# The mixer of a two-layer decoder trunk on one core: the spacing of the chains' steps on TensorE, the queue place of the transposed shares' copies, and the time at which gated outputs are turned

## The chip, the cores and the metric

The kernel runs on one core of a Trainium2 chip. The metric is device time in microseconds (us) of one execution; lower is better. The kernel before takes 2161.09 us, the median of three runs from 2160.48 to 2162.0.

## The reference

Two layers; x has 512 tokens of 1024 features, float32 throughout. Each layer is a feed-forward half-step, a mixer, and a second feed-forward half-step, each between RMS norms:

```python
for l in range(DEPTH):
    x = x + 0.5 * rms_norm(swiglu(rms_norm(x, gn[0]), w_gate, w_up, w_down), gn[1])
    proj = rms_norm(x, gn[2]) @ w_in[l]
    hq, hf, hi, hg, aq, ak, av, gate_a, gate_b = jnp.split(proj, IN_SPLITS, axis=-1)
    y_hg = hgrn2_mixer(hq, hf, hi, hg, lb_all[l], hgrn_head_gain[l]) @ w_branch_hgrn[l]
    y_at = swa_sink_attention(aq, ak, av, attn_sinks[l]) @ w_branch_attn[l]
    mixed = jax.nn.sigmoid(gate_a) * y_hg + jax.nn.sigmoid(gate_b) * y_at
    x = x + rms_norm(mixed @ w_out[l], gn[3])
    ...
```

`hgrn2_mixer` is a gated linear recurrence with four heads of 128 by 128 state; each head's output is divided by its own root mean square and multiplied by the SiLU of `hg`. `swa_sink_attention` is attention of eight heads over a window of 128 tokens with a distance penalty and a sink in the softmax; it is computed in four blocks of 128 queries. Only the mixer is touched by the change.

## The kernel before

Every large product is done in three TensorE products of a high and a low part (`mm3`), since one pass in the fast float32 format isn't exact enough. Weights arrive by DMA on SP's queue in tiles of 128 by 1024, ScalarE rounds the high part (`whi`, L228), and the low part (`wlo`) is made by VectorE (L235) or by an accumulating DMA on GpSimd's queue (L232, L233). Activations stay in SBUF in a pool of 61 slots named `s`. PSUM has eight banks: five named `acc` for the main stream, three named `aux` for the chains below. An `aux` bank can be written anew only when the last reader of the tile that held it is done.

**What sets the order.** TensorE's instructions stand in the order in which the code issues them. Those of the other engines are put in order by a scheduler when the program is built; each engine then works through its list in that order, and the order in the built program is the one that the chip runs.

In the mixer (`mixer`, L837) there is a main stream of projections and several chains that run beside it, written as generators. The main stream gives, in order: the projections for the first two recurrence heads (`quad`), the keys, queries and values of the attention, two token-major projections (`project_tok`: the recurrence's values `vs`, copied out at L991, and the out-gates `gs`, L995 to L998), the last two heads' projections, eight attention branches (`branch`), and then the recurrence branches (`branches`), the last of which ask for the whole of the attention (`attended`) and of the recurrence (`recurred`). The chains are four heads (`head`, its steps in `run` and `recurrence_scores`) and two attention chains, which take blocks 0 and 2, and 1 and 3 (`attend`).

`Order` keeps an estimated TensorE time `t`: `mm` and `transpose` add to it. A chain yields a number of ns from the table `WAIT` when it must wait for other engines; after each weight block of the main stream (`wmm`: three products) `poll` steps every chain that is due. `until` steps the chains without any main product between, while a result is missing.

The steps that the prediction names:

- An attention block: scores on TensorE (12 products of 64 rows per step, two steps); VectorE adds the distances (L925), reduces the maximum (L930, L932) and prepares the softmax (L934, L936); ScalarE takes eight exponentials (L942) with their sums `den`; VectorE inverts `den` (L946, L947) and scales the shares (L950, four instructions). Then for each of up to two key blocks eight TensorE transposes fill two `aux` banks (L111), ScalarE copies both out (L963), and after both key blocks four products use the copies as moving operands (L104, `aux<-s,s` with 64 columns); L972 and L974 split the result.
- A head's end: ten products of 128 by 128 into one `aux` bank, ScalarE squares (L866), VectorE sums (L868), ScalarE takes the root (L869), VectorE inverts (L870) and scales out of the bank (L872). After `norm` ns the gates are multiplied in (L877, four instructions of 128 by 128), after `gate` ns four transposes turn the gated output.

```python
    po = aux()
    for t in range(TT):
        for s in range(t + 1):
            mm(po[:, t * P : (t + 1) * P], block(s, t), vs[s][:, i * P : (i + 1) * P], s == 0, s == t)
    ...
    yield WAIT["gate"]
```

- Ahead of a head's end, two products make its last cross-chunk scores (`s2`), which ScalarE copies out (L825) and which the head's end then reads; the time between is `blocks` (350 ns).
- `sums` (L451, then L353 to L356 and the split at L303 and L304) prepares sums of quarters of the input for the faster products of the later branches; VectorE does the sums, ScalarE the high parts.

Of the kernel before, what the change touches and what calls it, by code (L numbers as in the profile page):

```python
# [30 lines left out]

WAIT = dict(
    early=0.0, first=0.0, spread=2300.0, squares=1700.0, lay=34500.0, laid=770.0, normed=6300.0, final=2600.0,
    head=2600.0, diag=0.0, level=1720.0, chunks=1270.0, blocks=350.0, norm=2370.0, gate=4500.0,
    values=1200.0, scores=2000.0, exp=9000.0, shares=4500.0, turn=1900.0, lent=31000.0, apart=4000.0, block=2000.0, pair=4000.0, att0=1260.0, att1=12300.0,
)
W32, WS, AHEAD, TAIL, PLAIN, FIRST, EARLY, LATE = 4, 6, 3, 2, 4, 7, 4, 8
HEADS = (0, 4, 1, 5, 2, 6, 3, 7)


@with_exitstack
def trunk(ctx: ExitStack, tc: tile.TileContext, xin, wall, gains, lbT, hgain, sinks, c_dist, c_mask, c_ident, out):
    nc = tc.nc
# [11 lines left out]
    def nm(s):  # L55
        seq[0] += 1
        return f"{s}_{seq[0]}"

    def big(dt=F32, shape=None):
        return sb.tile(shape or [P, S], dt, tag="s", name=nm("s"), bufs=SLOTS)  # L60
# [7 lines left out]
    def aux():  # L68
        return ps.tile([P, S], F32, tag="aux", name=nm("aux"), bufs=3)
# [6 lines left out]
    class Order:  # L76
        def __init__(self):
            self.t = 0.0
            self.cos = []

        def spawn(self, gen, delay=0.0):
            self.cos.append([self.t + delay, len(self.cos), gen])

        def step(self, c):
            self.t = max(self.t, c[0])
            try:
                wait = next(c[2])
                c[0] = self.t + wait
            except StopIteration:
                self.cos.remove(c)  # L90

        def poll(self):
            for c in [c for c in self.cos if c[0] <= self.t]:
                self.step(c)

        def until(self, cond):
            self.poll()
# [29 lines left out]
    p = aux()  # L127
# [488 lines left out]
    def project_tok(pre):  # L616

        o = [acc() for _ in range(TT)]
        for k in range(KT):
            b = ws.next(4, TT)  # L620
            for tt in range(TT):
                mm3(o[tt], cut(pre.h[k], slice(tt * P, (tt + 1) * P)), b[2:], k == 0, k == KT - 1)
                ws.used(b)
                order.poll()
        return o
# [211 lines left out]
    def mixer(l, pre, nxt):  # L837
# [69 lines left out]
        def attend(n):  # L907
            K = 256 if n else P
            k0 = (n - 1) * P if n else 0
            qc = slice(n * P, (n + 1) * P)  # L910
            mxs = small([P, NH], "mxs")
            sc = {}
            for j in range(2):

                pe = [aux() for _ in range(2)]
                for h in range(2):
                    for e in range(2):
                        r = slice(e * HD, (e + 1) * HD)
                        o, i, kc = pe[e][:, h * 256 : h * 256 + K], 2 * j + h, slice(k0, k0 + K)
                        mm3(o, [t[r, qc] for t in qS[i]], [t[r, kc] for t in kS], True, True)  # L920
                for e in range(2):
                    s = sc[j, e] = big(F32, [P, 2, 256])
                    for h in range(2):
                        i = 4 * j + 2 * h + e
                        nc.vector.scalar_tensor_tensor(  # L925
                            s[:, h, :K], dist[:, 256 - K :], 2.0 ** -(HEADS[i] + 1), pe[e][:, h * 256 : h * 256 + K],
                            op0=ALU.mult, op1=ALU.add,
                        )
                    i = 4 * j + e
                    nc.vector.tensor_reduce(mxs[:, i : i + 3 : 2], s[:, :, :K], axis=AX.X, op=ALU.max)  # L930
                yield WAIT["scores"]
            nc.vector.tensor_tensor(mxs, mxs, sink[:, l, :], op=ALU.max)  # L932
            neg = small([P, NH], "neg")
            nc.vector.tensor_scalar(neg, mxs, -1.0, None, op0=ALU.mult)  # L934
            es = small([P, NH], "es")
            nc.vector.tensor_tensor(es, sink[:, l, :], mxs, op=ALU.subtract)  # L936
            nc.scalar.activation(out=es, in_=es, func=AF.Exp)
            den = small([P, NH], "den")
            for (j, e), s in sc.items():
                for h in range(2):  # L940
                    i = 4 * j + 2 * h + e
                    nc.scalar.activation(  # L942
                        out=s[:, h, :K], in_=s[:, h, :K], func=AF.Exp, bias=neg[:, i : i + 1], accum_out=den[:, i : i + 1]
                    )
            yield WAIT["exp"]
            nc.vector.tensor_tensor(den, den, es, op=ALU.add)  # L946
            nc.vector.reciprocal(den, den)  # L947
            for (j, e), s in sc.items():
                i = 4 * j + e
                nc.vector.tensor_tensor(  # L950
                    s[:, :, :K], s[:, :, :K], den[:, i : i + 3 : 2].unsqueeze(2).to_broadcast([P, 2, K]), op=ALU.mult
                )
            yield WAIT["shares"]
            nk = K // P
            pt = {}
            for b in range(nk):
                pe = [aux() for _ in range(2)]
                for e in range(2):
                    for i in range(4):
                        transpose(pe[e][:, i * P : (i + 1) * P], sc[i // 2, e][:, i % 2, b * P : (b + 1) * P])  # L960
                for e in range(2):
                    t = pt[b, e] = big()
                    nc.scalar.copy(t, pe[e])  # L963
                yield WAIT["turn"]

            po = aux()
            for b in range(nk):
                for e in range(2):
                    v0 = (n - nk + 1 + b) * P + e * HD
                    mm(po[e * HD : (e + 1) * HD, :], va[:, v0 : v0 + HD], pt[b, e], b == 0, b == nk - 1)  # L970
            for k in range(4):
                nc.scalar.copy(bhi[k][:, qc], po[:, k * P : (k + 1) * P])  # L972
            for k in range(4):
                nc.vector.tensor_tensor(  # L974
                    blo[k][:, qc], po[:, k * P : (k + 1) * P], bhi[k][:, qc].bitcast(F32), op=ALU.subtract
                )
            left[0] -= 1
# [8 lines left out]
        order.spawn(attention((1, 3)), WAIT["att1"])  # L986


        for p in project_tok(pre):
            v = big()  # L990
            nc.scalar.copy(v, p)  # L991
            vs.append(v)
        for p in project_tok(pre):
            g = big()
# [56 lines left out]
    for l in range(DEPTH):  # L1051
        for n in (0, 2, 4):
# [5 lines left out]
            else:  # L1058
                p = FIRST if l + n == 0 else PLAIN
# [4 lines left out]
    pre = First()  # L1064
# [65 lines left out]
    for l in range(DEPTH):  # L1130
        pre = ffn(l, 0, pre, (l, 2), halves=l > 0)
        pre = mixer(l, pre, (l, 4))
        pre = ffn(l, 4, pre, (l + 1, 0) if l + 1 < DEPTH else None)
# [4 lines left out]
def _layout(inputs):  # L1138
# [15 lines left out]
    for l in range(DEPTH):  # L1154
        for n in ("ffn1", None, "ffn2"):
# [6 lines left out]
            fq = np.stack([hf.reshape(D, H, P), hq.reshape(D, H, P)], 2).reshape(D, 1024)  # L1162
            aq = w[:, 2048:2560].reshape(D, NH, HD)[:, list(HEADS)].reshape(D, 512)
            ak, av = w[:, 2560:2688], w[:, 2688:2816]
# [50 lines left out]
```

## Time and profile before

| | |
|---|---|
| median of three runs | 2161.09 us |
| the profiled execution's own time | 2161.84 us |
| its span, first to last instruction | 2160.0 us |
| TensorE busy | 2138.8 us (99%) |
| VectorE busy | 1438.1 us (67%) |
| ScalarE busy | 1065.1 us (49%) |

The mixer of the first layer takes about 374 to 600 us of the span, that of the second about 1443 to 1670 us. In the timeline a row gives start, length, engine, line, operation, output and inputs, shapes and count, and in brackets the idle time ahead of it with what ended it. A TensorE product of 512 columns is drawn 0.39 us long, but the next one starts 0.23 us after it, so an idle time as listed is about 0.16 us shorter than the time lost.

### The profile page before, as it was taken

How to read it: one execution, taken by the hardware profiler on the slowest of the kernel's cores; microseconds unless marked ns; L12 is line 12 of the kernel's file. 1: busy time of each engine (PE TensorE's matmuls, PEld its weight loads, DVE VectorE, ACT ScalarE, POOL GpSimd, SP SyncE). 2: the span in 40 equal slices, each digit the busy share in tenths (PEclk: the TensorE clock that was granted, in tenths of full speed). 3: DMA queues.
4: the chain of work that ended last, by engine and by line, in shares of the span. 5: the costliest groups of instructions: out<-in, count | busy, mean ns of one | idle time of the engine just before them, and what ended most of it. 6: DMA issues, size and time to landing. Idle time of an engine off the chain costs nothing. (4 is left out here: it accounts for less than half of the span.)

```text
span 2160.0 us, 34431 instructions
## 1 busy us (share of the span) xinstructions
PE 2138.8 (99%) x13389; PEld 1918.3 (89%) x13389; DVE 1438.1 (67%) x2501; ACT 1065.1 (49%) x1752; POOL 138.0 (6%) x164
## 2 busy tenths in 40 slices
PE   9999999999999999999999999999999999999998
PEld 8899988877888999998899998898778989999987
DVE  5877725856776777783477776268667757777823
ACT  7555615445445555562355555253554546555622
POOL 0011000000000011110001110000000000111000
PEclk9999999999999999999999999999999999999999
DMA  8677833221146357774337777332112463677731
GB/s 249 151 185 175 223 101 117 79 69 59 60 107 205 117 124 182 183 198 144 107 104 179 176 175 207 98 118 78 59 59 69 114 196 110 147 181 185 200 117 39
DMA packets 144563, 294.26 MB, mean 136 GB/s; under 512 B 15408, under 2 KB 73232, under 8 KB 144400
## 3 DMA queue, kind: packets, MB, share of 16 engines
q1 hardware_dynamic: 121216, 228.31, 32.4%
q0 software_dynamic: 23040, 63.71, 17.1%
q8 instruction: 105, 1.72, 0.3%
q14 instruction: 58, 0.48, 0.1%
q10 hardware_dynamic: 144, 0.05, 0.0%
HBM read 213.58 MB, written 14.73 MB: 106 GB/s over the span
## 5 line engine op out<-in xcount | busy, mean ns | idle before, releaser
L104 PE MATMUL acc<-s,whi 128*128 128x256 f32 (+1 forms) x4968 | 1068.6, 312 | 0.7 <-DVE s L683 0.7
L104 PEld LDWEIGHTS acc<-s,whi 128*128 128x128 f32 x4968 | 811.2, 191 | 47.5 <-issue 2.1
L104 PE MATMUL acc<-s,wlo 128*128 128x256 f32 (+1 forms) x2484 | 770.6, 310 | 0.1
L228 ACT CAST whi<-w 128x1024 fp32r<-128x1024 f32 (+1 forms) x373 | 350.7, 957 | 426.9 <-PE aux L104 256.3
L104 PEld LDWEIGHTS acc<-s,wlo 128*128 128x128 f32 x2484 | 474.3, 191 | 26.0 <-DVE wlo L235 0.4
L235 DVE TENSOR_TENSOR wlo<-w,whi 128x1024 fp32r<-128x1024 f32 (+1 forms) x213 | 258.7, 1217 | 325.3 <-ACT whi L228 321.3
L104 PE MATMUL acc<-whi,s 128*128 128x512 f32 x1296 | 424.8, 393 | 1.9 <-ACT s L991 1.9
L228 ACT CAST whi<-tt 128x1024 fp32r<-128x1024 f32 x154 | 161.4, 1048 | 341.8 <-DVE tt L222 196.8
L104 PEld LDWEIGHTS acc<-whi,s 128*128 128x128 f32 x1296 | 243.3, 188 | 59.6 <-issue 4.9
L233 POOL DMA_DIRECT2D wlo<-w x160 | 137.8, 863 | 1883.9 <-ACT wlo L232 1689.4
L235 DVE TENSOR_TENSOR wlo<-tt,whi 128x1024 fp32r<-128x1024 f32 x154 | 188.1, 1221 | 102.4 <-ACT whi L228 102.3
L104 PE MATMUL acc<-wlo,s 128*128 128x512 f32 x648 | 252.7, 390 | 0.0
L104 PE MATMUL aux<-s,whi 128*128 128x256 f32 x1232 | 225.2, 283 | 0.0
L104 PE MATMUL aux<-whi,s 128*128 128x512 f32 x624 | 207.9, 390 | 0.0
L104 PEld LDWEIGHTS aux<-s,whi 128*128 128x128 f32 x1232 | 192.2, 192 | 0.0
L104 PE MATMUL aux<-s,wlo 128*128 128x256 f32 x616 | 174.6, 284 | 1.7 <-DMA wlo<-w 1.6
L104 PEld LDWEIGHTS acc<-wlo,s 128*128 128x128 f32 x648 | 121.8, 188 | 23.5
L104 PEld LDWEIGHTS aux<-whi,s 128*128 128x128 f32 x624 | 117.2, 188 | 24.2
L232 ACT ACTIVATE wlo<-w 128x1024 fp32r<-128x1024 f32 (+1 forms) x160 | 129.7, 844 | 0.0
L104 PE MATMUL aux<-wlo,s 128*128 128x512 f32 x312 | 121.4, 389 | 0.0
L104 PEld LDWEIGHTS aux<-s,wlo 128*128 128x128 f32 x616 | 118.2, 192 | 2.2 <-DMA wlo<-w 2.2
L303 ACT CAST s<-s 128x512 fp32r<-128x512 f32 (+1 forms) x148 | 81.1, 599 | 50.9 <-DVE s L354 44.1
(161 smaller groups left out, 1899.2 us busy)
## 6 DMA issues: line engine op xcount, KB each, us to landing
w<-wall SPq DMA_DIRECT2D x267, 512.0 KB, 3.5
w<-wall SPq DMA_DIRECT2D x352, 128.0 KB, 2.8
wlo<-w POOLq DMA_DIRECT2D x83, 512.0 KB, 5.5
wlo<-w POOLq DMA_DIRECT2D x77, 256.0 KB, 3.3
x_d<-s SPq DMA_DIRECT2D x48, 256.0 KB, 2.0
s<-x_d SPq DMA_DIRECT2D x48, 256.0 KB, 4.7
w<-wall SPq DMA_DIRECT2D x34, 256.0 KB, 3.0
grow<-rows_d SPq DMA_DIRECT2D x6, 512.0 KB, 4.5
```

The source lines that it names most:

```text
L104: nc.tensor.matmul(o, lhsT, rhs, start=start, stop=stop)
L228: i = nc.scalar.copy(it.hi[:, c], w[:, c])
L232: nc.scalar.mul(it.lo[:, c], w[:, c], -1.0)
L233: nc.gpsimd.dma_start(it.lo[:, c].bitcast(F32), w[:, c], accum_op=ALU.add)
L235: nc.vector.tensor_tensor(it.lo[:, c], w[:, c], it.hi[:, c].bitcast(F32), op=ALU.subtract)
L303: nc.scalar.copy(hi, src)
```

## The change

It has four parts.

1. **Spacing.** After a chain's step has put work on TensorE, no other chain is stepped by `poll` until `t` has grown by `rest`, 1200 ns: six products of 512 columns by the estimate. One chain is stepped at a time, the one that is due longest.
2. **Copies of the transposed shares.** They are issued under `tc.high_priority(offset=PRIOR)` with `PRIOR` 400, which changes their place in ScalarE's list; and after the last key block the chain waits 3000 ns (`turned`) where it waited 1900 (`turn`).
3. **Gated outputs.** `gate` goes from 4500 to 8000 ns.
4. **Values.** Of the four copies of `vs`, two go to VectorE (`tensor_copy`), the others stay on ScalarE.

```diff
-    head=2600.0, ..., norm=2370.0, gate=4500.0,
-    values=1200.0, ..., turn=1900.0, lent=31000.0, ...
+    head=2600.0, ..., norm=2370.0, gate=8000.0,
+    values=1200.0, ..., turn=1900.0, turned=3000.0, rest=1200.0, lent=31000.0, ...
+PRIOR = 400
...
         def step(self, c):
-            self.t = max(self.t, c[0])
+            t = self.t = max(self.t, c[0])
             try:
                 wait = next(c[2])
                 c[0] = self.t + wait
             except StopIteration:
                 self.cos.remove(c)
+            if self.t > t:
+                self.rest = self.t + WAIT["rest"]

         def poll(self):
-            for c in [c for c in self.cos if c[0] <= self.t]:
-                self.step(c)
+            while self.t >= self.rest:
+                ready = [c for c in self.cos if c[0] <= self.t]
+                if not ready:
+                    break
+                self.step(min(ready, key=lambda c: c[0]))
...
-                    t = pt[b, e] = big()
-                    nc.scalar.copy(t, pe[e])
-                yield WAIT["turn"]
+                    pt[b, e] = big()
+                with tc.high_priority(offset=PRIOR):
+                    for e in range(2):
+                        nc.scalar.copy(pt[b, e], pe[e])
+                yield WAIT["turn" if b < nk - 1 else "turned"]
...
-        for p in project_tok(pre):
+        for i, p in enumerate(project_tok(pre)):
             v = big()
-            nc.scalar.copy(v, p)
+            (nc.vector.tensor_copy if i % 2 else nc.scalar.copy)(v, p)
```

In the changed kernel the lines lie 7 to 10 further down: L963 is L973, L866 to L872 are L874 to L880, L942 to L950 are L950 to L958, L995 to L998 are L1005 to L1008.

**First place: block 2's shares.** On ScalarE before, in the first layer, the copies of the second pair of banks of a block stand right behind block 3's exponentials, and the root of the first head (`ss`) stands behind them:

```order
L942 ACTIVATE s_5037,den_5071<-s_5037,neg_5066 128x256 x2
L942 ACTIVATE s_5041,den_5071<-s_5041,neg_5066 128x256 x2
L963 COPY s_5096<-aux_5086 128x512
L963 COPY s_5098<-aux_5087 128x512
L972 CAST s_4502<-aux_5115 128x128
L972 CAST s_4503<-aux_5115 128x128
L972 CAST s_4504<-aux_5115 128x128
L972 CAST s_4505<-aux_5115 128x128
L866 ACTIVATE s_5142<-aux_5131 128x512
L869 ACT_TABLE_LOAD
L869 ACTIVATE ss_5144<-ss_5144,eps_t 128x4
```

On ScalarE now the exponentials of block 3 are cut by a root of the first head (with a table load on either side), and the copies of block 2's shares stand behind the gates and behind the root of the second head, `ss_5148`:

```order
L877 ACT_TABLE_LOAD
L877 ACTIVATE ss_5082<-ss_5082,eps_t 128x4
L950 ACT_TABLE_LOAD
L950 ACTIVATE s_5016,den_5100<-s_5016,neg_5095 128x256 x2
...
L874 ACTIVATE s_5146<-aux_5135 128x512
L236 CAST whi_5270<-w_845_4872 128x1024
L877 ACT_TABLE_LOAD
L877 ACTIVATE ss_5148<-ss_5148,eps_t 128x4
L973 COPY s_5177<-aux_5167 128x512
L973 COPY s_5178<-aux_5168 128x512
L973 COPY s_5204<-aux_5194 128x512
L973 COPY s_5205<-aux_5195 128x512
```

On VectorE now, the sum that this root needs stands behind block 3's `den`, one share and the eight instructions of the gates:

```order
L954 TENSOR_TENSOR den_5100<-den_5100,es_5097 128x8
L955 RECIPROCAL den_5100<-den_5100 128x8
L958 TENSOR_TENSOR s_5012<-s_5012,den_5100 128x512
L1006 SCALAR_TENSOR_TENSOR s_5115<-s_5115,acc_4774 128x512
L1006 SCALAR_TENSOR_TENSOR s_5119<-s_5119,acc_4775 128x512
L1008 TENSOR_TENSOR s_5115<-s_5115,hgh 128x512
L1008 TENSOR_TENSOR s_5119<-s_5119,hgh 128x512
L1006 SCALAR_TENSOR_TENSOR s_5123<-s_5123,acc_4776 128x512
L1006 SCALAR_TENSOR_TENSOR s_5127<-s_5127,acc_4777 128x512
L1008 TENSOR_TENSOR s_5123<-s_5123,hgh 128x512
L1008 TENSOR_TENSOR s_5127<-s_5127,hgh 128x512
L876 TENSOR_REDUCE ss_5148<-s_5146 128x4
```

On TensorE the order at this place has moved too. Before, both transposing steps of block 2 and its four products come ahead of the first two heads' ends (`aux_5131`, `aux_5153`). Now, behind block 3's last scores, there are nine main products, the first head's end (`aux_5069`, ten products), nine main products, the second head's end (`aux_5135`), nine main products, and then the two transposing steps with nine main products between them:

```order
L119 MATMUL aux_5167<-ident,s_4889 128x128 x2
L119 MATMUL aux_5167<-ident,s_4937 128x128 x2
L119 MATMUL aux_5168<-ident,s_4893 128x128 x2
L119 MATMUL aux_5168<-ident,s_4941 128x128 x2
...
L119 MATMUL aux_5194<-ident,s_4889 128x128 x2
L119 MATMUL aux_5194<-ident,s_4937 128x128 x2
L119 MATMUL aux_5195<-ident,s_4893 128x128 x2
L119 MATMUL aux_5195<-ident,s_4941 128x128 x2
```

With three `aux` banks, `aux_5194` takes the bank of `aux_5167`, and `aux_5195` that of `aux_5135`, the second head's end.

**Second place: the last head's end.** On ScalarE before, the copy of the last cross-chunk scores (L825) follows the copy at L818 directly:

```order
L303 CAST s_5752<-aux_5747 128x512
L818 COPY s_5777<-aux_5778 128x256
L825 COPY s_5792<-aux_5793 128x512
L228 CAST whi_5916<-w_983_5659 128x1024
L866 ACTIVATE s_5817<-aux_5806 128x512
```

Now two high parts of `sums` stand between (L311 was L303, L833 was L825):

```order
L826 COPY s_5816<-aux_5817 128x256
L236 CAST whi_5961<-w_991_5714 128x1024
L311 CAST s_5846<-s_5840 128x512
L311 CAST s_5850<-s_5841 128x512
L833 COPY s_5858<-aux_5859 128x512
```

and on VectorE now the sums `s_5840` and `s_5841` that they round come behind a branch's gate (L1022) and a low part (L243):

```order
L825 TENSOR_SCALAR s_5484<-s_5484,s_5513 128x128
L459 TENSOR_TENSOR s_5836<-s_3703,s_3704 128x512
L1022 SCALAR_TENSOR_TENSOR s_5804<-s_5804,acc_5806 128x512
L459 TENSOR_TENSOR s_5838<-s_3729,s_3730 128x512
L243 TENSOR_TENSOR wlo_5962<-w_991_5714,whi_5961 128x1024
L361 TENSOR_TENSOR s_5840<-s_5838,s_5836 128x256
L364 TENSOR_TENSOR s_5841<-s_5836 128x256
L362 SCALAR_TENSOR_TENSOR s_5840<-s_5840,s_5836 128x256
L363 SCALAR_TENSOR_TENSOR s_5841<-s_5840,s_5838 128x256
```

On TensorE six main products, not three, now stand between the two products of `s2` (`aux_5859`) and the head's end (`aux_5869`). The second layer has the same rows with other numbers. The lists of SP's and GpSimd's queues are the same in both kernels.

More of the change, by code (lines that the diff above doesn't have):

```diff
@@ L33 @@
     early=0.0, first=0.0, spread=2300.0, squares=1700.0, lay=34500.0, laid=770.0, normed=6300.0, final=2600.0,
-    head=2600.0, diag=0.0, level=1720.0, chunks=1270.0, blocks=350.0, norm=2370.0, gate=4500.0,
-    values=1200.0, scores=2000.0, exp=9000.0, shares=4500.0, turn=1900.0, lent=31000.0, apart=4000.0, block=2000.0, pair=4000.0, att0=1260.0, att1=12300.0,
+    head=2600.0, diag=0.0, level=1720.0, chunks=1270.0, blocks=350.0, norm=2370.0, gate=8000.0,
+    values=1200.0, scores=2000.0, exp=9000.0, shares=4500.0, turn=1900.0, turned=3000.0, rest=1200.0, lent=31000.0, apart=4000.0, block=2000.0, pair=4000.0, att0=1260.0, att1=12300.0,
 )
 W32, WS, AHEAD, TAIL, PLAIN, FIRST, EARLY, LATE = 4, 6, 3, 2, 4, 7, 4, 8
+PRIOR = 400
 HEADS = (0, 4, 1, 5, 2, 6, 3, 7)
@@ L78, in __init__ @@
             self.t = 0.0
+            self.rest = 0.0
             self.cos = []
```

## The prediction

> **What bounds the kernel now.** I read the page's engine shares first, then what TensorE waited for, then the timeline at each of these waits.
>
> ```profile
> span 2160.0 us, 34431 instructions
> PE 2138.8 (99%) x13389; PEld 1918.3 (89%) x13389; DVE 1438.1 (67%) x2501; ACT 1065.1 (49%) x1752; POOL 138.0 (6%) x164
> ```
>
> TensorE is busy for 99% of the span, so nothing that shortens VectorE's or ScalarE's work counts in itself. The change adds and removes no product. It can only take away or add time in which TensorE stands. The list of TensorE's waits, in us in total, times and the longest:
>
> ```profile
> PE aux L111 <- DVE s L877: 4.2, 2, 2.1
> PE aux L104 <- ACT s L963: 3.1, 4, 1.2
> PE acc L104 <- ACT s L991: 1.9, 2, 1.0
> PE aux L104 <- DVE s L754: 0.8, 2, 0.4
> ```
>
> The reader is to see that parts 2, 3 and 4 of the change each aim at one row: gated outputs (L877), copies of shares (L963), copies of values (L991). Their 8 waits are 9.2 us as listed. A wait as listed is shorter than what it costs, as the timeline shows:
>
> ```profile
> 514.38 0.40 PE L104 MATMUL acc<-s,wlo 128*128 128x512 f32 x1
> 516.88 0.85 PE L111 MATMUL aux<-ident,s 128*128 128x128 f32 x4 [2.10 <-DVE s L877]
> 520.36 0.71 PE L104 MATMUL acc<-s,whi 128*128 128x512 f32 x2
> ...
> 1585.95 0.84 PE L111 MATMUL aux<-ident,s 128*128 128x128 f32 x4 [2.10 <-DVE s L877]
> 1590.86 0.71 PE L104 MATMUL acc<-s,whi 128*128 128x512 f32 x2
> ```
>
> From 514.38 to 516.88 pass 2.50 us where 0.24 would do: 2.26 lost for 2.10 listed, 0.16 more. So the 8 waits cost 9.2 + 8 x 0.16 = **10.5 us**, and the whole possible gain is little more than that, 0.5%. One further cost stands in the same rows: the same work, from those transposes to the product at the end, takes 520.36 - 516.88 = 3.48 us in the first layer and 1590.86 - 1585.95 = 4.91 in the second, 1.4 us more. The windows (last but two column: granted clock) say why:
>
> ```profile
> 517.00:520.00 3.00, 3.00 (x19) 2.32 (x19) 3.00 (x9) 1.18 (x2) 0.00 (x0) 1.00 0.00 0
> 1587.00:1590.30 3.30, 3.30 (x13) 2.60 (x12) 2.65 (x5) 1.01 (x2) 0.00 (x0) 0.50 0.23 66
> ```
>
> After one of the two 2.1 us waits the clock was granted at half for some 3.3 us; after the other it wasn't. A long wait has an after-cost of 1.4 us, sometimes.
>
> **What goes.** `gate` at 8000 ns lets the gated outputs be turned 3.5 us later, more than the 2.26 us that they came too late; two of four value copies run on VectorE beside ScalarE's, so that the `acc` banks come free earlier; the transposes of block 2's shares no longer wait for their copies with TensorE idle at the products. I take all 8 waits as gone, -10.5 us, and with them the clock's fall in the second layer, -1.4. The order shown with the change doesn't let me expect these waits at their old places.
>
> **What comes, first place: block 2's transposes.** The order shows what now stands where. Spacing has put the second transposing step (`aux_5194`) behind two heads' ends, and it needs a bank that is freed by the copy `s_5177`. That copy is behind the root `ss_5148`, which needs a sum on VectorE behind the gates. Both sides start at the same point, T0, the end of block 3's last scores. TensorE's side, from rows of before for the same pieces:
>
> ```profile
> 491.92 0.50 PE L104 MATMUL acc<-whi,s 128*128 128x512 f32 x1
> 492.74 1.04 PE L111 MATMUL aux<-ident,s 128*128 128x128 f32 x8
> 493.53 0.48 PE L104 MATMUL acc<-whi,s 128*128 128x512 f32 x1
> ...
> 495.67 1.03 PE L111 MATMUL aux<-ident,s 128*128 128x128 f32 x8
> ...
> 502.41 2.39 PE L104 MATMUL aux<-s,s 128*128 128x128 f32 x20
> 504.56 0.47 PE L104 MATMUL acc<-whi,s 128*128 128x512 f32 x1
> ```
>
> Nine main products take 495.67 - 493.53 = 2.14 us (0.24 each), a head's end 504.56 - 502.41 = 2.15, eight transposes 493.53 - 492.74 = 0.79. TensorE is at `aux_5194` at T0 + 4 x 2.14 + 2 x 2.15 + 0.79 = **T0 + 13.65**. The other side runs over VectorE and ScalarE:
>
> ```profile
> 492.02 1.08 DVE L925 SCALAR_TENSOR_TENSOR s<-dist,aux 128x256 f32<-128x256 f32 x3 [1.17 <-PE aux L104]
> 495.06 0.16 DVE L936 TENSOR_TENSOR es<-sink,mxs 128x8 f32<-128x8 f32 x1
> 499.64 0.17 DVE L946 TENSOR_TENSOR den<-den,es 128x8 f32<-128x8 f32 x1 [2.82 <-ACT s L942]
> 500.08 2.50 DVE L950 TENSOR_TENSOR s<-s,den 128x512 f32<-128x512 f32 x4
> 505.53 0.69 DVE L868 TENSOR_REDUCE ss<-s 128x4 f32<-128x512 f32 x1 [2.12 <-ACT s L866]
> 507.42 0.69 DVE L872 TENSOR_TENSOR s<-aux,ss 128x512 f32<-128x512 f32 x1
> 511.64 1.28 DVE L996 SCALAR_TENSOR_TENSOR s<-s,acc 128x512 f32<-128x512 f32 x2
> 512.85 1.28 DVE L998 TENSOR_TENSOR s<-s,hgh 128x512 f32<-128x512 f32 x2
> 516.45 1.29 DVE L877 TENSOR_TENSOR s<-s,s 128x128 f32<-128x128 f32 x6
> ...
> 495.46 0.21 ACT L937 ACTIVATE es<-es 128x8 f32<-128x8 f32 x1
> 499.51 1.04 ACT L963 COPY s<-aux 128x512 f32<-128x512 f32 x2
> 505.52 1.28 ACT L869 ACT_TABLE_LOAD   x1
> 506.81 0.30 ACT L869 ACTIVATE ss<-ss,eps_t 128x4 f32<-128x4 f32 x1
> ```
>
> - Scores to `es`: 491.92 to 495.22 (end of L936) before, 3.3 us. Now three share instructions of block 2 stand between, 0.605 each (four last 2.50, the first 0.69): T0 + 5.1.
> - The exponentials: from 495.22 to `den` at 499.64 are 4.4 us. Now a load, the root and a second load cut them: 1.29 (505.52 to 506.81) + 0.2 + 1.29 = 2.8. T0 + 12.3.
> - VectorE: `den` to the first share 0.44, that share 0.605, eight gate instructions at 0.605 (512.85 - 511.64 is two of them) 4.84, the sum 0.69: T0 + 18.9.
> - ScalarE: the root 0.3, the copy 0.55, and about 0.1 for the two hand-overs: T0 + 19.8.
>
> So TensorE stands 19.8 - 13.65 = **6.1 us**. Then come four transposes (0.4 us, T0 + 20.2), and `aux_5195` needs the bank that the second head's L872 reads: on VectorE four L877 (0.2 each), two shares, the reciprocal (0.1), one more share and L872 (0.69) stand behind the sum, 18.9 + 0.8 + 1.2 + 0.1 + 0.6 + 0.7 = T0 + 22.3: another **2.1 us**. 8.2 us per layer, 16.4 in all. Behind it on ScalarE stand the remaining copies and a high part, for products that are over two us of main stream away. Bounds: at least 5 us per layer, if both table loads and the small steps were hidden (8.2 - 2.8 - 0.4); at most 11, if VectorE came to the scores as late as it did before (its idle row ahead of L925 says it was 1.17 us early; a low part of 1.2 us may stand there).
>
> **Second place: the last head's end.** It reads the copy of `s2`, now behind two high parts that wait for VectorE's sums.
>
> ```profile
> 578.48 0.60 PE L104 MATMUL aux<-s,s 128*128 128x128 f32 x4
> 580.30 1.02 PE L104 MATMUL aux<-s,s 128*128 128x256 f32 x4
> 580.98 0.81 PE L104 MATMUL acc<-s,whi 128*128 128x512 f32 x2
> ...
> 578.90 0.28 DVE L816 TENSOR_SCALAR s<-s,s 128x128 f32<-128x128 f32 x1
> ...
> 590.46 0.42 DVE L353 TENSOR_TENSOR s<-s,s 128x256 f32<-128x256 f32 x1
> ...
> 592.60 0.42 DVE L355 SCALAR_TENSOR_TENSOR s<-s,s 128x256 f32<-128x256 f32 x1
> ...
> 581.36 0.59 ACT L825 COPY s<-aux 128x512 f32<-128x512 f32 x1 [1.87 <-PE aux L104]
> ```
>
> Count from the products ahead (578.48). TensorE: 2.50 to the end of the two `s2` products, six main products 1.43, three products of the head's end that need no `s2` 0.65: 4.6 us. VectorE begins 0.42 later, four column scalings 0.8, two sums and a gate 1.8, then a low part and three quarter sums (590.46 to 592.60, the same four) 2.14: 5.2; ScalarE's two high parts and the copy 0.59 + 2 x 0.5: 6.8, 6.85 with the hand-over. **2.3 us** per layer, 4.6 in all. Bounds 0 (before, with three main products fewer, nothing waited here) to 2.9 (the high parts each drawn in full).
>
> **Priced at nothing.** L754's row (0.8 us): the heads' level steps are regrouped, and two steps of the same head pair still meet on VectorE; between a gain of 0.8 and a loss of 2.8 (a low part of 1.2 ahead of one wait in each layer) I stay at 0, the nearest row. SP's and GpSimd's lists are the same, so weights come as before. The two values on VectorE add two copies of 0.7 per layer, under main products that VectorE's 67% leaves room for; without that cover it would be at most 2.8 us. The one table load more per layer lies in the 8.2.
>
> **The clock.** After the first place, in both layers, TensorE has done four transposes in 8.6 us: I take a fall each, 2 x 1.4. At the second place 2.3 us is like the two waits of before, one fall in two: 2 x 0.7. Together +4.2, less the 1.4 that goes: +2.8. Bounds: 0, and 4 us more if the clock stays low for two spells.
>
> The Trainium skill, "TensorE: Matmul & The Clock Gate", section "Part 1: The HAM clock gate (the "warmup" mystery)", has the clock at half after an idle window of about 3.4 us; the trace shows a fall after 2.1 us of idle, so the measurement decides. By the page's rule the second place would cost no clock, and the estimate would be 1.4 us less.
>
> **Sum.** -10.5 + 16.4 + 4.6 + 2.8 = +13.3 us on the profiled execution's 2161.84 us (2160.0 of span and 1.84 around it), 2175.1; that execution lies 0.75 above the median, so 2174.4, and I say **2174 us**, 0.6% slower. The measurement of this kernel tells about 0.2% (4.3 us) from no change.
>
> **Rivals.**
> - The waits go and none comes: -10.5 - 1.4, **2149 us**, faster. This is decided at one point, whether `s_5177` is done by T0 + 13.65. It needs 6.1 us off that chain: the eight gate instructions (4.84) and one load (1.29) would have to be out of it. For it speaks that the spacing gives each step more cover elsewhere; against it, that the built lists hold root, gates and copy in this sequence and each engine takes its list in sequence (VectorE's eight gate instructions in a row ahead of L877 made the 2.1 us wait of before). 8%.
> - The chain at the first place is shorter by the bounds, 5 us per layer, the second place doesn't wait, and there is one fall each: -10.5 + 10 + 1.4 = +0.9, **2162 us**, the same within 0.2%. 10%.
> - Table loads cost more than their rows: two in the chain at the first place. If each held ScalarE 1.38 us longer, the wait would be 2.8 longer per layer, +5.5: **2180 us**. The row speaks against it, since the root starts 0.01 us after the load's end. The Trainium skill, "ScalarE: Activation LUTs", section "What ACT_TABLE_LOAD costs", has 1283 ns for the load and about 1380 ns of drain on top; the trace agrees with the first and shows no drain. With the clock staying low for two spells this is the upper case. 7%.
>
> **Chances and range.** Forecast 75%, rivals 8, 10 and 7%. Faster 0.08, the same 0.09, slower 0.83. The forecast's own bounds give 2166 (clock and second place at their low ends) to 2180; with part of the middle rival the range is **2164 to 2180**.
>
> **What would show it.** In the list of TensorE's waits the rows for L877, L963 and L991 are gone; in their place stands `aux` at the transposes' line waiting for the share copies (L973) with about 6 us twice, then for L880 (L872 before) with about 2, and `aux` at the products' line waiting for L833 (L825 before) with about 2.2 twice. The clock windows behind the first place show 0.5. I am wrong if the first of these rows is under 3 us, or if TensorE's waits in the mixer sum to less than before.

## The result and the profile after

The changed kernel takes **2175.0 us** (median of four runs, 2173.32 to 2177.17), the kernel before beside it 2161.55 (2160.48 to 2165.31). The ratio is 1.006 with a 95% interval of 1.0042 to 1.0077: 0.6% slower. The forecast was 2174 us, in a range of 2164 to 2180.

The page of the changed kernel, first lines: TensorE is busy 0.9 us longer, the span is 13.1 us longer.

```profile
span 2173.1 us, 34425 instructions
PE 2139.7 (98%) x13389; PEld 1920.8 (88%) x13389; DVE 1440.0 (66%) x2505; ACT 1065.6 (49%) x1750; POOL 138.4 (6%) x164
```

The list of what TensorE waited for, changed kernel (us in total, times, the longest):

```profile
PE aux L119 <- ACT s L973: 11.7, 2, 5.9
PE aux L112 <- ACT s L833: 4.1, 2, 2.0
PE aux L112 <- DVE s L762: 3.2, 2, 1.6
PE aux L119 <- DVE s L880: 2.7, 2, 1.4
```

The rows for gated outputs, copies of shares at the products and copies of values are gone. The four that stand in their place are the forecast's three (L973, L833, L880), each once in a layer, and one that it had priced at nothing: L762, the masked level steps, 0.8 us in total before (L754) and 3.2 now.

The first place, in the first layer, on TensorE:

```profile
505.82 0.39 PE L112 MATMUL acc<-s,wlo 128*128 128x512 f32 x1
512.08 1.12 PE L119 MATMUL aux<-ident,s 128*128 128x128 f32 x4 [5.87 <-ACT s L973]
514.55 1.12 PE L119 MATMUL aux<-ident,s 128*128 128x128 f32 x4 [1.36 <-DVE s L880]
```

and on VectorE and ScalarE at the same time:

```profile
504.70 0.17 DVE L954 TENSOR_TENSOR den<-den,es 128x8 f32<-128x8 f32 x1 [3.40 <-ACT s L950]
...
505.75 1.28 DVE L1006 SCALAR_TENSOR_TENSOR s<-s,acc 128x512 f32<-128x512 f32 x2
...
509.34 1.29 DVE L1008 TENSOR_TENSOR s<-s,hgh 128x512 f32<-128x512 f32 x2
510.54 0.68 DVE L876 TENSOR_REDUCE ss<-s 128x4 f32<-128x512 f32 x1
```

```profile
508.02 1.28 ACT L877 ACT_TABLE_LOAD   x1
511.26 0.30 ACT L877 ACTIVATE ss<-ss,eps_t 128x4 f32<-128x4 f32 x1 [1.95 <-DVE ss L876]
511.46 1.05 ACT L973 COPY s<-aux 128x512 f32<-128x512 f32 x2
```

The reader sees the forecast's chain link by link: `den`, one share, the eight gate instructions (505.75 to 510.6), the sum, the root at 511.26, the copy (the first of two, done near 512.03), and TensorE's transposes 0.05 us later. TensorE was ready at 505.82 + 0.23 = 506.05.

The cost of this on the clock, in stretches of 3.41 us. A row gives the stretch, its length, TensorE's busy time with its instructions, the granted clock (1.00 is full speed, 0.50 half), and the share and rate of the DMA:

```profile
506.27:509.68 3.41, 0.00 (x0) 1.00 0.00 0
509.68:513.09 3.41, 1.01 (x4) 0.50 0.00 0
513.09:516.51 3.42, 2.06 (x8) 0.50 0.00 0
516.51:519.92 3.41, 3.41 (x10) 0.50 0.52 160
519.92:523.33 3.41, 3.41 (x16) 1.00 0.44 148
```

Ten instructions where the next stretch has sixteen: the clock stayed at half for 10.24 us, not for one spell of 3.4 us.

### The profile page after: what moved, and what is told of

It is laid out like the page before. It is cut to its first block, busy times and chain, and to the rows that moved or that the text cites. A ratio compares the mean times of both kernels' runs of the same rounds, so it can differ in the third digit from the quotient of the medians.

```text
span 2173.1 us, 34425 instructions
## 1 busy us (share of the span) xinstructions
PE 2139.7 (98%) x13389; PEld 1920.8 (88%) x13389; DVE 1440.0 (66%) x2505; ACT 1065.6 (49%) x1750; POOL 138.4 (6%) x164
## 4 chain that ended last, share of the span: by engine, by line
PE 92%; DVE 4%; ACT 2%; issue 1%; DMA 0%; POOL 0%; ACTq 0%; DVEq 0%; POOLq 0%
PE acc L112 68%; PE aux L112 23%; PE aux L119 1%; DVE s L486 1%; DVE wlo L243 1%; DMA wlo<-w 0%; DVE s L573 0%; ACT s L950 0%; PE acc L119 0%; ACT whi L236 0%; ACT s L498 0%; DVE s L561 0%; DVE s L1008 0%; DVE s L1006 0%; DVE s L565 0%
## 5 line engine op out<-in xcount | busy, mean ns | idle before, releaser
L112 PE MATMUL acc<-s,whi 128*128 128x256 f32 (+1 forms) x4968 | 1073.3, 313 | 1.2 <-DVE s L691 0.7
L112 PEld LDWEIGHTS acc<-s,whi 128*128 128x128 f32 x4968 | 812.9, 192 | 50.3 <-issue 3.7
L112 PE MATMUL acc<-s,wlo 128*128 128x256 f32 (+1 forms) x2484 | 772.0, 311 | 0.2
L112 PEld LDWEIGHTS acc<-s,wlo 128*128 128x128 f32 x2484 | 475.4, 191 | 26.7 <-DVE wlo L243 0.4
L243 DVE TENSOR_TENSOR wlo<-w,whi 128x1024 fp32r<-128x1024 f32 (+1 forms) x213 | 258.9, 1218 | 323.3 <-ACT whi L236 320.9
L112 PE MATMUL acc<-whi,s 128*128 128x512 f32 x1296 | 424.2, 393 | 0.0
L112 PEld LDWEIGHTS acc<-whi,s 128*128 128x128 f32 x1296 | 243.3, 188 | 55.1 <-issue 3.2
L243 DVE TENSOR_TENSOR wlo<-tt,whi 128x1024 fp32r<-128x1024 f32 x154 | 188.1, 1222 | 98.5 <-ACT whi L236 98.3
L112 PE MATMUL acc<-wlo,s 128*128 128x512 f32 x648 | 252.5, 390 | 0.0
L112 PE MATMUL aux<-s,whi 128*128 128x256 f32 x1232 | 225.1, 283 | 0.0
L112 PE MATMUL aux<-whi,s 128*128 128x512 f32 x624 | 207.9, 390 | 0.0
L112 PEld LDWEIGHTS aux<-s,whi 128*128 128x128 f32 x1232 | 192.2, 192 | 0.0
L112 PE MATMUL aux<-s,wlo 128*128 128x256 f32 x616 | 174.5, 283 | 1.7 <-DMA wlo<-w 1.7
L112 PEld LDWEIGHTS acc<-wlo,s 128*128 128x128 f32 x648 | 121.7, 188 | 24.0
L112 PEld LDWEIGHTS aux<-whi,s 128*128 128x128 f32 x624 | 117.1, 188 | 24.1
L112 PE MATMUL aux<-wlo,s 128*128 128x512 f32 x312 | 121.4, 389 | 0.0
L112 PEld LDWEIGHTS aux<-s,wlo 128*128 128x128 f32 x616 | 118.3, 192 | 2.1 <-DMA wlo<-w 2.1
L311 ACT CAST s<-s 128x512 fp32r<-128x512 f32 (+1 forms) x148 | 81.3, 599 | 60.3 <-DVE s L362 57.6
```

Of the source, the lines that this page charges most:

```text
L112: nc.tensor.matmul(o, lhsT, rhs, start=start, stop=stop)
L243: nc.vector.tensor_tensor(it.lo[:, c], w[:, c], it.hi[:, c].bitcast(F32), op=ALU.subtract)
L311: nc.scalar.copy(hi, src)
```

## The experiments

The theory: the spacing makes the four new waits, by the order that it gives TensorE's list; the other parts take the waits of before away. The rivals: the new waits come from the priority or from the values on VectorE, or from two parts together.

### 1. The changed kernel without spacing

```diff
-            if self.t > t:
-                self.rest = self.t + WAIT["rest"]
...
-            while self.t >= self.rest:
-                ...
+            for c in [c for c in self.cos if c[0] <= self.t]:
+                self.step(c)
```

> The changed kernel without its first part: chains are stepped as before, the other three parts stay. Theory A (the spacing makes the new waits, the other parts take the old ones away): none of the four new rows (L973, L833, L762, L880 after the change) and none of the rows for gated outputs, copies of shares and copies of values; 2161.8 - 10.5 - 1.4 = 2149 to 2151 us. Rival B (the priority copies and the values on VectorE are what holds the transposes up): a wait of about 6 us for the share copies stays in each layer, 2165 us or more. Rival C (spacing was worth something against the waits of before): the waits at the share products stay, about 2156 us.

Measured: 2145.95 us, ratio to before 0.993 (0.9916 to 0.9943). In its list of TensorE's waits nothing of the chains is left but the level steps:

```profile
PE aux L105 <- DVE s L755: 0.8, 2, 0.4
```

Theory A holds in kind, B and C fall. The time is 3 us below what was expected, so the waits of before were dearer than the prediction had them. The products of shares show where: eight products in a row, in this kernel, and the same eight before.

```profile
479.36 1.94 PE L105 MATMUL aux<-s,s 128*64 128x512 f32 x8
481.23 0.50 PE L105 MATMUL acc<-whi,s 128*128 128x512 f32 x1
```

```profile
480.35 1.08 PE L104 MATMUL aux<-s,s 128*64 128x512 f32 x4
482.65 1.55 PE L104 MATMUL aux<-s,s 128*64 128x512 f32 x4 [1.22 <-ACT s L963]
484.13 0.50 PE L104 MATMUL acc<-whi,s 128*128 128x512 f32 x1
```

The eight take 1.87 us here and took 3.78: 1.91 lost, where the listed idle time is 1.22. These four products are drawn long over short gaps, and part of the wait is hidden in the drawing.

### 2. The changed kernel with the old wait behind the last key block

```diff
-turned=3000.0
+turned=1900.0
```

> The changed kernel with the wait behind the last key block at 1900 ns as before; spacing, priority, gate and values stay. Theory A as the prediction put it (the spacing alone puts the transposing steps behind two heads' ends): the 5.9 us wait for the share copies stays, 2172 to 2176 us. Rival D (it takes spacing and the later end of a block together; with 1900 ns TensorE's list has the steps in another order): no wait at block 2's second transposing step, no wait at the last head's end; some 3.8 us per layer at the products of shares, and the wait for the masked level steps as in the changed kernel; with a clock spell each about 2159 to 2164 us.

Measured: 2159.98 us, ratio to before 0.9995 (0.9987 to 1.0004), no difference. TensorE's waits:

```profile
PE aux L112 <- ACT s L973: 7.9, 2, 3.9
PE aux L112 <- DVE s L762: 3.2, 2, 1.6
```

Rival D is right about the waits: the one at block 2's transposes (`aux` at L119) is gone, one of 3.9 us at the products of shares (L112) has come, and the last head's end doesn't wait. TensorE's list shows what has moved. The two heads' ends start at 494.85 and 500.72, block 2's two transposing steps at

```profile
498.47 1.04 PE L119 MATMUL aux<-ident,s 128*128 128x128 f32 x8
...
504.40 1.04 PE L119 MATMUL aux<-ident,s 128*128 128x128 f32 x8
```

and on ScalarE the second root and the copies of the second step at

```profile
510.63 0.30 ACT L877 ACTIVATE ss<-ss,eps_t 128x4 f32<-128x4 f32 x1
510.84 1.05 ACT L973 COPY s<-aux 128x512 f32<-128x512 f32 x2
```

The second transposing step (504.40) stands behind both heads' ends here too, and its copies stand behind the second root (510.63), so the products that read them wait. The first step (498.47) now lies between the two heads' ends; its copies run early, at 500.98, and its banks are free in time. Experiment 5, with nothing but the spacing, has the same order (494.99 to 504.52), so the spacing alone puts the second step and its copies late. The wait at the transposes needs the later end of a block as well, which puts the first step behind the second head's end. In this company 3000 in place of 1900 costs 2175.0 - 2160.0 = 15 us.

### 3. The changed kernel with all values on ScalarE

```diff
-            (nc.vector.tensor_copy if i % 2 else nc.scalar.copy)(v, p)
+            nc.scalar.copy(v, p)
```

> The changed kernel with all four copies of values on ScalarE again. As the prediction put it (the values on VectorE free the acc banks earlier): the waits of 1.13 us at the main products for a copy of values come back in each layer, 2177 us. Rival (those waits went because the order moved, not because of the engine; TensorE's list is the same as in the changed kernel): no such wait, 2175 us, the same as the changed kernel.

Measured: 2175.65 us, ratio to before 1.0064 (1.0051 to 1.0076), as the changed kernel. No wait for a copy of values came back; the same four rows stand in the list, with the same 11.7, 4.1, 3.2 and 2.7 us. The values' engine does nothing for the time here.

### 4. The changed kernel with the head's sum moved ahead on VectorE

```diff
-                nc.vector.tensor_reduce(ss, ...)
+                with tc.high_priority(offset=PRIOR): nc.vector.tensor_reduce(ss, ...)
```

> The changed kernel with the sum of a head's squares (L876) given priority, which moves it on VectorE from behind eight gate instructions to behind three. Theory A (the copy waits for the root, the root for the sum, the sum for the gates): the wait for the share copies falls in each layer from 5.87 us to about 3.9: the squares end 1.0 us after TensorE gets there (507.07 against 506.05), the sum could end at 507.8, and then the second root's table load (508.02 to 509.30) decides, the root and the copy end at 510.1; with one clock spell perhaps shorter 2168 to 2171 us. Rival (ScalarE's own list or the table loads hold the copy, not the gates): the wait stays at 5.8 to 6.0 us, 2175 us.

Measured: 2170.19 us, ratio to before 1.0042 (1.003 to 1.0055). TensorE's wait, and ScalarE's rows ahead of its end:

```profile
510.09 1.11 PE L119 MATMUL aux<-ident,s 128*128 128x128 f32 x4 [3.93 <-ACT s L973]
```

```profile
506.91 1.05 ACT L236 CAST whi<-w 128x1024 fp32r<-128x1024 f32 x1
507.97 1.28 ACT L877 ACT_TABLE_LOAD   x1
509.27 0.30 ACT L877 ACTIVATE ss<-ss,eps_t 128x4 f32<-128x4 f32 x1
509.47 1.05 ACT L973 COPY s<-aux 128x512 f32<-128x512 f32 x2
```

The wait fell from 5.87 to 3.93 us. The sum on VectorE runs from 507.49 to 508.17, ahead of the load's end. VectorE's gates did hold the copy, and taking five of them out of the chain gives 1.94 us, not the 3.0 that they last, because ScalarE's own list (a high part, then the table load) is next in line. The root starts 0.02 us after the load's end.

### 5. The kernel before with spacing alone

```diff
-turn=1900.0
+turn=1900.0, rest=1200.0
...
+            if self.t > t:
+                self.rest = self.t + WAIT["rest"]
...
+            while self.t >= self.rest:
+                ...
```

> The kernel before with the first part alone. Theory E (spacing's cost depends on what stands beside it): with 1900 ns behind the last key block the block 2 wait is the 4.1 us of turned_1900, the masked level steps wait 1.77 us, and the last head's end waits 2.2 us again, so about 4.4 us above turned_1900, with a clock spell 2164 to 2167 us. Rival A (spacing costs what undoing it in the changed kernel gave back, 29 us, whatever the other parts are): 2161.4 + 29 = 2190 us, less the waits of before that it moves, 2175 us at the least.

Measured: 2166.87 us, ratio to before 1.003 (1.0019 to 1.0041). TensorE's waits:

```profile
PE aux L111 <- ACT s L970: 7.9, 2, 4.0
PE aux L111 <- ACT s L832: 4.1, 2, 2.0
PE aux L111 <- DVE s L761: 3.2, 2, 1.6
```

Theory E holds, A in its additive form falls: the spacing costs 5.7 us on the kernel before and 29.1 us (2175.0 - 2145.95) beside the other parts. It also takes the waits of before for outputs and values away, without any help: none of their rows is here. The products of shares wait longer than before (7.9 us against 3.1 as listed).

### 6. The kernel before with `gate` at 8000 alone

```diff
-gate=4500.0
+gate=8000.0
```

> The kernel before with gate at 8000 ns alone. Theory: the two waits for gated outputs go (2.27 us each), and with them the clock's fall in the second layer (1.4 us), all others stay: 2161.4 - 4.5 - 1.4 = 2155.5, from 2154.5 to 2156.5 us. Rival (outputs turned later push the last head's or the branches' work into a new wait): 2158 us or more.

Measured: 2155.04 us, ratio to before 0.9972 (0.9963 to 0.9981). The row for gated outputs is gone; those for copies of shares (L963, 3.2 us in four waits) and of values (L991, 1.9 in two) are left.

The median is as expected: 6.1 us for two waits of 2.27 and the clock's fall, which is gone from the second layer's mixer. The profiled execution, the longest of its eleven (2157.19), has a fall elsewhere, at 1307.34, behind a wait of 2.30 us for weights between the layers (1.62 in the profile before), so a single execution tells less here than the median.

### 7. The kernel before with the two delays alone

```diff
-gate=4500.0
+gate=8000.0, turned=3000.0
...
-                yield WAIT["turn"]
+                yield WAIT["turn" if b < nk - 1 else "turned"]
```

> The kernel before with two numbers changed: 3000 ns behind the last key block and gate 8000 ns; no spacing, no priority, all values on ScalarE. Theory F (the two delays take the waits away, priority and the values' engine do nothing for the time): 2146 us, within 1.5 us of the kernel without spacing, and no wait for copies of values or of shares. Rival (priority takes the waits at the share products away, VectorE's copies those for values): the waits for values come back, 2148.5, or those for shares too, 2153 us or more.

Measured: 2145.96 us, ratio to before 0.9931 (0.9918 to 0.9943). Of the chains its list of waits has only the level steps, 0.8 us in total as before (L754). The two delays do all that the change gains; this kernel is as fast as the kernel without spacing (2145.95) and faster than both kernels of this case.

### 8. The changed kernel with `gate` at 4500

```diff
-gate=8000.0
+gate=4500.0
```

> The changed kernel with gate at 4500 ns again. Theory G (the wait at the last head's end, 2.2 us in each layer, needs the later turning of outputs as well as the spacing, since that moves six products and two high parts of sums there; with the spacing the outputs are not waited for even at 4500): that wait goes, the waits at block 2's transposes stay, 2175 - 4.4 - 1.4 = 2169 to 2171 us. Rival (the spacing alone makes the second place, and gate takes the waits for gated outputs away here too): 2175 us, or 2179 us where the waits for gated outputs come back.

Measured: 2169.05 us, ratio to before 1.0039 (1.0026 to 1.0051). The wait at the last head's end is gone, those at block 2's transposes stay, and no wait for gated outputs has come:

```profile
PE aux L119 <- ACT s L973: 11.8, 2, 5.9
...
PE aux L119 <- DVE s L880: 2.7, 2, 1.4
```

The time is as theory G has it, but its reason falls with experiment 5: there the same wait stands with `gate` at 4500 and 1900 behind the last key block. With spacing, the second place is there at (4500, 1900) and (8000, 3000), and isn't at (4500, 3000) and (8000, 1900). The first of these four is experiment 5, without the priority and with all values on ScalarE. Adding the priority there changes no built list, so the values' engine is its only other difference. As far as these four go, neither delay makes the second place alone; their combination decides which steps meet.

### 9. The kernel before with the priority alone

```diff
+                with tc.high_priority(offset=PRIOR):
+                    for e in range(2):
+                        nc.scalar.copy(pt[b, e], pe[e])
-                    nc.scalar.copy(t, pe[e])
```

> The kernel before with the priority of the share copies alone, 1900 ns behind the last key block. Theory: in this company (unlike in the changed kernel, where the built lists with and without priority are the same) priority takes the waits at the share products away, 1.9 + 0.9 + 0.3 us per layer, and leaves those for values (2 x 1.13) and for gated outputs (2 x 2.27) with the clock's fall: 2161.2 - 6.2 = 2155, from 2153 to 2157 us. Rival (priority does nothing): 2161 us.

Measured: 2154.43 us, ratio to before 0.9967 (0.9954 to 0.9979). Left are

```profile
PE aux L112 <- DVE s L878: 4.3, 2, 2.1
...
PE acc L105 <- ACT s L994: 1.9, 2, 1.0
```

Priority takes the waits at the share products away, and these were worth 6.6 us (2160.98 - 2154.43; 4.5 to 9.9 by the ratio's interval). In the changed kernel it does nothing: the lists built with `PRIOR` 400 and with 0 are the same on every engine there.

### 10. The kernel before with `turned` alone

```diff
-                yield WAIT["turn"]
+                yield WAIT["turn" if b < nk - 1 else "turned"]
```

> The kernel before with 3000 ns behind the last key block alone. Theory F (this delay moves the products of shares and what follows, so that shares, values and gated outputs are all ready, and gate adds little): no row for copies of shares or values, at most a small one for outputs; 2147 to 2150 us. Rival (each part takes its own row away): only the waits at the share products go, 2161.2 - 6.2 = 2155 us.

Measured: 2148.47 us, ratio to before 0.994 (0.9927 to 0.9952). The rows for copies of shares and of values are gone, of that for gated outputs a small one is left (L877, 0.5 us in total), and a new small one has come (L304, 0.6).

Theory F holds: one delay takes two kinds of wait away and nearly all of the third, 12.5 of the 15.2 us of experiment 7. That it does so by moving everything behind it is argued from the order, not shown by a run of its own. The parts don't own their rows: alone, priority gives 6.6, `gate` 6.1, `turned` 12.5, and the best of them together 15.

### 11. The changed kernel with half the spacing

```diff
-rest=1200.0
+rest=600.0
```

> The changed kernel with 600 ns of spacing, three products in place of six. Theory H (the new waits come from the order that six products of spacing give, in which block 2's transposing steps stand behind two heads' ends; with three they stand ahead): none of the four new waits, the masked level steps wait a little longer than in the kernel without spacing; 2146 to 2149 us. Rival (any spacing costs in proportion to it): half of the 29 us, about 2160 us.

Measured: 2148.57 us, ratio to before 0.9941 (0.9927 to 0.9955). TensorE's waits in the mixer are two rows, L762 (2.0 us in total, the masked level steps) and L856 (1.1). In the first layer block 2's first transposing step starts at 491.39; the second step and the first head's end are

```profile
494.34 1.03 PE L119 MATMUL aux<-ident,s 128*128 128x128 f32 x8
...
497.27 2.39 PE L112 MATMUL aux<-s,s 128*128 128x128 f32 x20
```

Theory H holds: both transposing steps stand ahead of the first head's end. Three products of spacing cost two to three us against none (2148.57 and 2145.95), six cost 29: not a price in proportion, but a change of order between the two.

## Why the prediction was right, and where it was wrong

The forecast was +13.3 us on the profiled execution, measured are +13.1 (2173.1 - 2160.0). What goes and what comes were both forecast too small, by 3.6 and 3.9 us. That the two errors cancel is luck; the sizes of the first and the second place, most of what comes, are not.

| term | predicted | measured | by |
|---|---|---|---|
| waits of before and the clock's fall, gone | -11.9 | -15.5 | 2145.95 - 2161.42, experiment 1 |
| of these the share products | -3.7 | -6.6 | experiment 9 |
| first place | +16.4 | 2 x (6.03 + 1.67) = +15.4 | timeline after |
| second place | +4.6 | 2 x 2.2 = +4.4 | 593.62 to 596.48, below |
| level steps (L754, now L762) | 0 | +2.4 | list: 3.2 - 0.8 |
| clock, what is left of 29.1 | +4.2 | +6.9 | 29.1 - 15.4 - 4.4 - 2.4 |

**First place: right, in mechanism and size.** T0 lies at 492.3 in the changed kernel (its first main product behind the last scores, L112 `acc<-whi,s`, starts at 492.31). The working had TensorE at T0 + 13.65 and the copy at T0 + 19.8; they came at 506.05 (T0 + 13.7) and 512.03 (T0 + 19.7). `den` had been put at T0 + 12.3 and started at 504.70, T0 + 12.4. Experiment 4 shows that the gates are in the chain and the table load is the next bound. The second wait was 1.67 us lost, not 2.1. Inside the chain two small errors cancelled: `es` was done at T0 + 4.7, not 5.1, and from there to `den` passed 7.7 us, not 7.2.

**Second place: right.** 2.86 us from the first row's start to the second's, of which its six instructions at 0.11 take 0.66 (three products, in two instructions each). Counted from the products ahead, which start at 589.54 now, TensorE stands from 4.7 us on (forecast 4.6) and the copy is done at 6.9 (6.85); the copy L833 stands behind the two high parts and they behind the sums, as said.

```profile
593.62 0.83 PE L112 MATMUL aux<-s,s 128*128 128x128 f32 x6
596.48 1.83 PE L112 MATMUL aux<-s,s 128*128 128x128 f32 x14 [2.04 <-ACT s L833]
```

```profile
594.81 1.14 ACT L311 CAST s<-s 128x512 fp32r<-128x512 f32 x2 [3.11 <-DVE s L362]
595.85 0.58 ACT L833 COPY s<-aux 128x512 f32<-128x512 f32 x1
```

**What goes: the size was wrong.** "So the 8 waits cost 9.2 + 8 x 0.16" took what one wait of 512-column products hides in its drawing for all of them. At the share products the hidden part is 0.69 for one wait (experiment 1), and some lost time there has no bracket at all: before, the four products at 463.07 take 1.48 us, half of the undisturbed eight would be 0.94. Together it is 6.6 us where 3.7 had been set.

**What goes: a reason was wrong.** "Two of four value copies run on VectorE beside ScalarE's, so that the acc banks come free earlier": experiment 3 has the same time without it, and experiments 5 and 10 have those waits gone with all values on ScalarE. The order of the steps took them away. Likewise "the transposes of block 2's shares no longer wait for their copies" holds, but by `turned` and the spacing; priority changes no list in the changed kernel.

**"Spacing has put the second transposing step behind two heads' ends": half the cause.** The sentence is right, and experiment 2 has the step there with the spacing alone. But the bank that it needs comes late only because the first step stands behind the second head's end too, and that takes the later end of a block (experiment 2). The forecast was made from the built order, which holds both, so its time didn't suffer.

**Priced at nothing: the level steps.** "I stay at 0, the nearest row" failed; the upper bound of 2.8 us held, with 2.4. The spacing does it by itself (3.2 us in experiment 5, 0.8 as before in experiments 1, 6, 7 and 10). In the changed kernel VectorE stands idle for 2.42 us for a high part, makes its low part (L243, from 401.71, 1.23 us), and then works without a pause to the end of TensorE's wait at 406.41; in the second layer it is the same from 1477.79. So this low part is the likely reason, as in the prediction's upper bound. No run moves it, and the cause stays open.

**The clock: too short.** A fall at each first place was right, and one of two at the second place as well, but a spell at the first place lasted 10.24 us, since the wait behind it (1.67 us) kept TensorE from a full stretch. The prediction had a longer spell only in a bound and in a rival. The 6.9 us in the table are what is left over by subtraction; the windows at half hold 15.6 us of busy time in the profiled execution, and half of that, 7.8 us, is an estimate of the same loss.

Of the rivals, the one without new waits (2149 us) isn't this kernel but the one without spacing: 2145.95. The one on table loads fell: in experiment 4 the load ends at 509.25 and the root starts at 509.27.

## What to carry to other kernels

When a planner's delay or spacing is changed, the waits belong to the order that comes out and not to the line that was edited: read the built lists at the places where a bank must come free, add up both sides from one common start, and price the later side's in-order list link by link. Price a wait that goes by the undisturbed duration of the same group of instructions elsewhere in the trace, not by its bracket. And try the parts of a change alone: here two delays (`turned` and `gate`) gave all of a gain of 0.7%, and the spacing turned it into a loss of 0.6%.

## What the runs showed of the hardware

Why one of two equal waits lets the clock fall wasn't known when the prediction was made. In every profiled run the granted clock changes on a grid of 3.413 us: in the changed kernel at 509.68, 519.92, 1673.63 and 1677.04, 3 windows, 341 and 342 windows behind the first. What counts is how much of one such window TensorE was busy. The second place in the first layer, where the wait of 2.2 us is cut by a window's edge, and in the second, where most of it lies in one:

```profile
595.01:598.43 3.42, 1.95 (x16) 1.00 0.36 137
598.43:601.84 3.41, 3.41 (x17) 1.00 0.00 0
```

```profile
1670.21:1673.63 3.42, 1.49 (x13) 1.00 0.50 153
1673.63:1677.04 3.41, 3.41 (x11) 0.50 0.00 0
```

The same holds for the two waits for gated outputs: before, the second layer's fell; with priority alone (experiment 9) the same waits of 2.3 us stand, and it is the first layer's:

```profile
510.78:514.19 3.41, 1.27 (x8) 1.00 0.00 0
514.19:517.60 3.41, 3.41 (x12) 0.50 0.18 35
```

```profile
1575.74:1579.15 3.41, 1.80 (x12) 1.00 0.16 64
1579.15:1582.57 3.42, 2.89 (x18) 1.00 0.00 0
```

In these rows a window with 1.49 us busy or less is followed by half the clock, one with 1.80 or more is not. Over the windows of all thirteen profiles the border is blurred: 1.38 us or less was followed by half each time and 1.65 or more never, while of those between, 1.49 and 1.63 (experiment 5, from 1309.62) were, and 1.48, 1.50, 1.54 and 1.57 were not. Drawn busy time is then near to what counts, but not quite it. The way back needs more: windows at half with up to 2.65 us busy left the clock there (2.06 in the table above, 2.65 in experiment 2), and 2.72 (experiment 5) or more brought it back. So a wait of less than some 1.7 us (3.41 - 1.65 = 1.76), alone in its window, cost no clock in these runs, one of 2.2 did by the luck of the grid, and those of about 4 and 6 us each did.

The Trainium skill, "TensorE: Matmul & The Clock Gate", section "Part 1: The HAM clock gate (the "warmup" mystery)", has a free-running activity window of 4096 cycles, which it gives as 3413 ns; the grid here agrees with it. Its rule of a whole idle window for the fall doesn't hold here: a window busy for 1.49 of 3.42 us was enough.
